# A 90 degree rotation in fp32: which engine makes the outputs of the first and the last macro tile

## Chip, cores, metric

One core of a Trainium2 chip. The metric is device time in microseconds (us) of one execution, the median of several runs. The core has TensorE (PE), VectorE (DVE), ScalarE (ACT), GpSimd (POOL), SyncE (SP) and 16 DMA engines.

## What is computed

```python
def setup_inputs():
    return {"x": np.random.randn(8192, 8192).astype(np.float32), "k": 1}

def reference(x, k):
    return np.rot90(x, k)
```

`out[i, j] = x[j, 8191 - i]`: a transpose with the order of the rows turned round. Nothing is calculated; 268 MB are read and 268 MB are written.

## The kernel before

**Tiling.** The input is cut into 16 macro tiles `kk` of 1024 rows (R) by 4096 columns (W). A macro tile has eight loads `t`, each 128 rows by 4096 columns (2 MB, load number `m = 8 kk + t`), and eight outputs `j`, each made of the 512 columns of chunk `j` of all eight loads (2 MB, output number `n = 8 kk + j`, stored as 512 rows by 1024 columns). Output `n` needs all eight loads of its macro tile.

**Stages.**
1. A load lands in one of five buffers. The first five loads use all five; after load 8 loads alternate between buffers 0 and 1 (`load_buf`), and the other three (2, 3, 4) are for outputs (`out_buf`). Loads 0 to 9 are issued by SP and ACT, all later ones by SP, each when DVE has turned the load that held its buffer before (`load_in_turn`, `taken`).
2. DVE turns the load into `ring`, which holds one macro tile, with the columns of each chunk in reverse order. Chunks that TensorE will transpose are copied (`tensor_copy`). The others are transposed in blocks of 32x32 (DVE's `transpose`, STREAM_TRANSPOSE in the profile). The last chunk of the last load (the corner) finds no slot in `ring`; it is turned into the landing buffer, and TensorE always transposes it. `pieces` lists in which portions and in what order DVE turns each load.
3. Outputs are made in one of two ways. `by_pe(kk)` names those that TensorE makes: 32 transposes of 128x128 into PSUM (two halves, `ps0` and `ps1`), which ACT copies into an output buffer. The others are `moved`: the 32x32 blocks are transposed already, and what is left are 16 copies that carry each row quadrant to its place (`moves`, `pairs`). DVE makes three of them (BY_DVE), POOL eight (BY_POOL) and ACT five; each is 32 partitions by 1024 elements.
4. ACT issues the store.

**Order.** Every engine has a fixed program, and the engines meet only in semaphores. DVE's program goes by loads: before it turns load `m` it makes its copies of output `n = m - 8`, if that is moved, and then waits for all of POOL's and its own copies of `n` (`s_pool`, `s_dve`), or for TensorE's transposes of `n` (`s_half`), since the load takes the places of output `n` in `ring`. POOL makes its eighth copy only when ACT has made all of its own (`s_act`). ACT stores a moved output when DVE has turned the first piece of load `n + 8`. An output buffer is written again only when its last store is done (`room_for`).

Macro tiles 1 to 12 (DVE, TensorE: 2 to 13) are played in a hardware loop two at a time, so in the profile most instructions have the line of a helper (L101, L104).

**Who makes what, before.** In macro tile 0 and in the last one, 15, TensorE makes all eight outputs. In macro tiles 1 to 13 it makes outputs 0 and 4, in 14 it makes 0, 2, 4, 6 and 7.

In the last macro tile no load follows that would need the ring, so the outputs are made in their order and ACT stores one after the other; outputs 120 and 121 are begun in halves before the last load is there (`FIRST`, `in_turn`).

Of the kernel before, what the change touches and what calls it, by code (L numbers as in the profile page):

```python
# [10 lines left out]
T = R // P  # L11
W = 4096
G = 4
J = W // (G * P)
# [7 lines left out]
Q = 32  # L22
BY_DVE = 3
BY_POOL = 8
BY_PE = [0, 4]
EARLY = range(T + 2)
BOTH = EARLY[-4:]
# [4 lines left out]
LAND = 2  # L32
OUTS = 3
# [140 lines left out]
def kernel(tc: tile.TileContext, x: bass.AP, k: bass.AP, out: bass.AP):  # L174
# [7 lines left out]
    KK = len(macros)  # L182
    n_out = KK * J
    n_load = KK * T
# [4 lines left out]
    wide = T // END  # L189
# [4 lines left out]
    outs = [(*o, [(j, g * P) for j in reversed(o[2]) for g in range(G)]) for o in outs]  # L194

    def by_pe(kk):
        if kk in (0, KK - 1):
            return list(range(J))
        return BY_PE if kk < KK - 2 else [*range(0, J, 2), J - 1]

    def in_quadrants(kk, j):
# [7 lines left out]
    for n, (kk, ts, js, blocks) in enumerate(outs):  # L209
# [5 lines left out]
        if kk < KK - 1 and js[0] == J - 1:  # L215
            ends = [F // H, F // H + rows, F]
# [24 lines left out]
    def moved_until(n):  # L241
        return sum(moved[: n + 1])
# [28 lines left out]
    def load_buf(m):  # L271
        if m < T:
            return m % (LAND + OUTS)
        return LAND + 2 if m == T else (m - T - 1) % LAND

    def out_buf(n):
        e = n - (KK * J - J)
        if e < 0:
            return LAND + (START if n < J else TURN[n // J % 2])[n % J]
        ends = [load_buf(n_load - 2)]  # L280
        ends += [LAND + i for i in reversed(range(OUTS))]
        ends += [load_buf(n_load - 1)]
        return ends[e % len(ends)]

    def once(e):
# [44 lines left out]
    for m in range(n_load):  # L330
        kk, t = divmod(m, T)
        here = by_pe(kk)
        rest = [j for j in range(J) if j not in here]
        if kk == KK - 1:
            got = [here] if t < T - 1 else [here[:wide], here[wide:-1], here[-1:]]
        elif t < T - 1:
            got = [here, rest]
        else:
            inner = [j for j in here if 0 < j < J - 1]
            got = [here[:1], [j for j in rest if j < J - 1], [J - 1], inner]  # L340
        got = [part for js in got for part in split(js)]
        pieces[m] = got
        for js in got:
            done += 1
            for j in js:
                rev[m, j] = done
# [6 lines left out]
    def landed(b, js):  # L353
        return at(bufs[b][:], (js[0] + 1) * CH - 1, [*strides(js, CH), [-1, CH]])

    def chunk(kk, t, js):
        if (kk, t, js[0]) == (KK - 1, T - 1, J - 1):
            return at(ring[:], 0, [[CH, 1], [1, CH]])
        places = [slot(kk, t, j) for j in js]
        assert max(places) < SLOTS  # L360
        return at(ring[:], places[0] * CH, [*strides(places, CH), [1, CH]])

    def moves(n, share):
        kk, ts, (j,), _ = outs[n]
        rows = len(ts) * P
        places = [slot(kk, t, j) for t in ts if (t, j) != (T - 1, J - 1)]
        ((step, tiles),) = strides(places, CH)
        for a, q in share:
            yield (
                at(  # L370
                    bufs[out_buf(n)][q * Q : q * Q + Q, :],
                    a * Q,
                    [[rows, G], [P, tiles], [1, Q]],
                ),
                at(
                    ring[a * Q : a * Q + Q, :],
                    places[0] * CH + q * Q,
                    [[P, G], [step, tiles], [1, Q]],
                ),
            )  # L380

    pairs = [(a, q) for a in range(P // Q) for q in range(P // Q)]

    def load(e, m, queue):
        r0, c0 = macros[m // T]
# [24 lines left out]
    def turned_in(n):  # L410
        kk, _, (j,), _ = outs[n]
        return rev[kk * T + T - 1 - (j == J - 1), j]
# [8 lines left out]
    def by_gpsimd(e):  # L421
        e.part(-1)
        e.memset(ident, 0.0).then_inc(s_id, 1)
        e.wait_ge(s_id, 1)
        e.affine_select(
            out=ident,
            in_=ident,
            compare_op=mybir.AluOpType.not_equal,
            fill=1.0,
            base=0,  # L430
            pattern=[[-1, P]],
            channel_multiplier=1,
        ).then_inc(s_id, 1)
        wait = once(e)
        for n, (kk, _, js, _) in enumerate(outs):
            e.part(kk)
            if moved[n]:
                room_for(wait, n)
                wait(s_rev, turned_in(n))
                for c, (to, of) in enumerate(moves(n, pairs[BY_DVE : BY_DVE + BY_POOL])):  # L440
                    if c == BY_POOL - 1:
                        wait(s_act, moved_until(n))
                    i = e.tensor_copy(out=to, in_=of)
                i.then_inc(s_pool, 1)

# [4 lines left out]
    def by_vector(e):  # L450
        wait = once(e)
        for m in range(n_load):
            kk, t = divmod(m, T)
            e.part(kk)
            b = load_buf(m)
            n = m - T
            if n >= 0 and moved[n]:
                room_for(wait, n)
                wait(s_rev, turned_in(n))
                for to, of in moves(n, pairs[:BY_DVE]):  # L460
                    i = e.tensor_copy(out=to, in_=of)
                i.then_inc(s_dve, 1)
            e.wait_ge(s_land[b], landings(m))
            if n >= 0:
                if moved[n]:
                    e.wait_ge(s_pool, moved_until(n))
                    e.wait_ge(s_dve, moved_until(n))
                else:
                    e.wait_ge(s_half, turned_until(n))
            for js in pieces[m]:  # L470
                if (m, js[0]) == (n_load - 1, J - 1):
                    e.wait_ge(s_half, turned_until(KK * J - J))
                if kk < KK - 1 and (t, js[0]) == (T - 1, J - 1):
                    wait(s_rev, rev[m, 0])
                    e.tensor_copy(
                        out=at(bufs[b][:], 0, [[CH, 1], [1, CH]]), in_=landed(b, js)
                    ).then_inc(s_rev, 1)
                    continue
                turn = e.transpose if in_quadrants(kk, js[0]) else e.tensor_copy
                turn(out=chunk(kk, t, js), in_=landed(b, js)).then_inc(s_rev, 1)  # L480

    def in_turn():
        for n in parts:
# [55 lines left out]
    def by_scalar(e):  # L539
        e.part(-1)  # L540
        wait = once(e)
        e.wait_ge(s_id, 2)
        e.copy(scratch, ident[:, :1])
        for m in EARLY[LAND + OUTS :]:
            load_in_turn(e, m, nc.scalar)
        for n, (kk, ts, js, blocks) in enumerate(outs):
            e.part(kk)
            r0, c0 = macros[kk]
            rows = len(ts) * P
            b = out_buf(n)  # L550
            if moved[n] or tight(n) or n == FIRST[1] or (kk < KK - 1 and js[0] == J - 1):
                room_for(wait, n)
            todo = list(moves(n, pairs[BY_DVE + BY_POOL :])) if moved[n] else []
            for to, of in todo[:1]:
                e.copy(to, of)
            if kk < KK - 1 and js[0] == J - 1:
                e.wait_ge(s_corner, kk + 1)
                e.copy(
                    at(bufs[b][:], rows - P, [[rows, G], [1, P]]),
                    at(corner, 0, [[P, G], [1, P]]),  # L560
                ).then_inc(s_freed, 1)
            if moved[n]:
                for to, of in todo[1:]:
                    i = e.copy(to, of)
                i.then_inc(s_act, 1)
                e.wait_ge(s_rev, rev[n + T, pieces[n + T][0][0]])
            else:
                for k, h, cols in parts[n]:
                    e.wait_ge(s_half, k + 1)
                    run, deep = len(cols) * P, 1  # L570
                    if cols[-1] - cols[0] >= run:
                        run = P * sum(f // rows == cols[0] // rows for f in cols)
                        deep = len(cols) * P // run
                    e.copy(
                        at(bufs[b][:], cols[0], [[rows, deep], [1, run]]),
                        at(ps[h][:], 0, [[run, deep], [1, run]]),
                    ).then_inc(s_ev, 1)
                e.wait_ge(s_ev, turned_until(n))
            groups = len(blocks)
            top = M - c0 - js[0] * CH - groups * P  # L580
            left = r0 + ts[0] * P
            e.dma_start(
                out=Place(out, top, groups * P, left, rows),
                in_=bufs[b][:, : groups * rows].rearrange("m (g f) -> m g f", f=rows),
            ).then_inc(s_store[b], 16)
# [50 lines left out]
```

## Time and profile before

| | |
|---|---|
| median of 3 runs (lowest, highest) | 1258.84 us (1258.72, 1259.64) |
| the profiled execution | 1259.08 us, of which 1257.8 us are the span of its instructions |
| DMA | 537.09 MB, 427 GB/s over the span |
| busy: DVE, POOL, ACT, PE | 63%, 59%, 48%, 24% of the span |
| loads | 128 of 2 MB (SP's queue q1, ACT's queue q10) |
| stores | 128 of 2 MB (ACT's queue q10), 15.8 us from issue to landing in the middle |

The page of the profile gives busy time by engine, then the span in 40 slices of 31.4 us, then the DMA queues, then the chain of work that ended last, followed back from the last instruction. "<-" names what ended an engine's idle time. In a row of the timeline the first number is the start and the second the time from the start of the group's first instruction to the end of its last, both in us; "x3" is how many instructions it merges; idle time before it stands in brackets. In a row of stretches the columns are: length, busy time of each engine with its instructions, TensorE's granted clock, DMA share (1 is all 16 DMA engines busy) and GB/s.

### The profile page before, as it was taken

What the parts mean: (1) busy time and instruction counts of PE and PEld (TensorE: products, weight loads), DVE (VectorE), ACT (ScalarE), POOL (GpSimd) and SP (SyncE); (2) the same over time, 40 slices, a digit from 0 to 9 for tenths busy, and PEclk for the clock granted to TensorE, in tenths of its full rate; (3) what the DMA queues carried; (4) which work ended last, traced back from release to release, by engine and by line L of the source; (5) the groups of instructions that cost most, each with busy time, mean ns of one, the idle gap of its engine ahead of it and who ended that gap; (6) DMA issues with size and microseconds to landing.
All of it is one profiled execution on the core that took longest, in us unless ns stands there. A gap on an engine that the chain in (4) does not pass through costs nothing.

```text
span 1257.8 us, 6012 instructions
## 1 busy us (share of the span) xinstructions
PE 302.9 (24%) x1556; PEld 264.8 (21%) x1556; DVE 793.8 (63%) x535; ACT 599.6 (48%) x556; POOL 744.0 (59%) x654
## 2 busy tenths in 40 slices
PE   1555013130131301313022130221302213024273
PEld 0454012130121301212012120121202212024273
DVE  2544866668666676666867667676677766764410
ACT  0334364463644636446364453645535455355364
POOL 0001966668666686666956668576685766965500
PEclk9987556555555555555556555565555556555597
DMA  9999999999999999999999999999999999999999
GB/s 400 420 430 429 429 429 429 429 431 430 430 430 429 430 428 430 428 430 430 430 430 429 431 428 431 428 430 428 430 430 429 430 429 431 427 423 428 427 428 381
DMA packets 36946, 537.09 MB, mean 427 GB/s; under 512 B 4160, under 2 KB 4160, under 8 KB 4160
## 3 DMA queue, kind: packets, MB, share of 16 engines
q10 hardware_dynamic: 19184, 278.93, 52.2%
q1 hardware_dynamic: 17744, 257.96, 48.0%
q8 instruction: 7, 0.11, 0.0%
q14 instruction: 11, 0.09, 0.0%
HBM read 268.44 MB, written 268.44 MB: 427 GB/s over the span
## 4 chain that ended last, share of the span: by engine, by line
DMA 71%; DVE 14%; ACT 4%; POOL 4%; issue 3%; PE 2%; ACTq 0%; DVEq 0%; SPq 0%; POOLq 0%
DMA buf<-in_x_dram 57%; DMA out_dram<-buf 14%; DVE ring L104 14%; ACT buf L104 4%; POOL buf L104 4%; PE ps L104 2%; ACTq L104 0%; DVE buf L104 0%; DVEq L101 0%; SPq L391 0%; DVEq L145 0%; POOLq L101 0%; SPq L311 0%; POOLq L151 0%; SPq L419 0%
## 5 line engine op out<-in xcount | busy, mean ns | idle before, releaser
L104 POOL COPY buf<-ring 32x1024 f32<-32x1024 f32 (+1 forms) x648 | 743.3, 1147 | 440.4 <-DMA out_dram<-buf 244.2
L104 ACT COPY buf<-ring 32x1024 f32<-32x1024 f32 (+1 forms) x405 | 414.8, 1024 | 324.2 <-DVE ring L104 292.5
L104 PE MATMUL ps<-head,ring 128*128 128x128 f32 x1496 | 290.7, 372 | 889.4 <-ACT buf L104 535.8
L104 PEld LDWEIGHTS ps<-head,ring 128*128 128x128 f32 x1496 | 255.3, 197 | 921.5 <-ACT buf L104 548.7
L104 DVE COPY ring<-buf 128x1024 f32<-128x1024 f32 (+5 forms) x152 | 157.7, 1044 | 415.6 <-DMA buf<-in_x_dram 320.1
L104 DVE STREAM_TRANSPOSE ring<-buf 128x3072 f32<-128x3072 f32 (+2 forms) x125 | 358.0, 2872 | 0.0
L104 ACT COPY buf<-ps 128x2048 f32<-128x2048 f32 (+4 forms) x149 | 183.3, 1278 | 313.6 <-DMA out_dram<-buf 149.3
L104 DVE COPY buf<-ring 32x1024 f32<-32x1024 f32 (+1 forms) x243 | 289.5, 1192 | 2.2
L104 PE MATMUL ps<-head,buf 128*128 128x128 f32 x60 | 15.2, 401 | 46.3 <-DVE buf L104 46.3
L104 PEld LDWEIGHTS ps<-head,buf 128*128 128x128 f32 x60 | 9.7, 199 | 52.0 <-issue 44.6
L104 DVE COPY buf<-buf 128x512 f32<-128x512 f32 x15 | 5.8, 387 | 0.0
L104 ACT ACT_TABLE_LOAD x1 | 1.3, 1283 | 3.4 <-PEq L419 3.4
L104 POOL MEMSET head<- 128x128 f32 x1 | 0.2, 204 | 2.9 <-POOLq L419 2.9
L104 POOL TENSOR_SCALAR_AFFINE_SELECT head<-head 128x128 f32<-128x128 f32 x1 | 0.3, 293 | 0.2 <-POOL head L104 0.2
L617 POOL MEMSET const-float32-0.0<- 128x1 f32 x1 | 0.1, 98 | 0.2 <-issue 0.2
L104 ACT COPY head<-head 128x1 f32<-128x1 f32 x1 | 0.2, 191 | 0.0
L617 POOL MEMSET const-bfloat16-1.0<- 128x1 bf16 x1 | 0.1, 100 | 0.0
L617 POOL MEMSET const-uint8-127<- 128x1 uint8 x1 | 0.1, 100 | 0.0
L617 POOL MEMSET const-float32-1.0<- 128x1 f32 x1 | 0.1, 98 | 0.0
## 6 DMA issues: line engine op xcount, KB each, us to landing
out_dram<-buf ACTq DMA_DIRECT2D x128, 2048.0 KB, 15.8
buf<-in_x_dram SPq DMA_DIRECT2D x121, 2048.0 KB, 15.0
buf<-in_x_dram ACTq DMA_DIRECT2D x3, 2048.0 KB, 16.9
buf<-in_x_dram SPq DMA_DIRECT2D x4, 1024.0 KB, 16.1
buf<-in_x_dram ACTq DMA_DIRECT2D x4, 1024.0 KB, 16.4
```

The lines of the kernel that those rows point to most:

```text
L104: i = getattr(e, self.name)(*self.args, **kwargs)
L617: nc = _bacc.Bacc("TRN2", target_bir_lowering=False, num_devices=1)
```

## The change

In macro tile 0 TensorE makes outputs 0 and 4 instead of all eight. In the last macro tile it makes outputs 0, 1, 3, 5 and 7; outputs 2, 4 and 6 become moved ones. For these three the 16 copies are shared out differently: DVE six, POOL six, ACT four. DVE makes them after its last load. POOL's last copy waits for ACT's and for DVE's, and ACT's store waits for POOL's. In the last macro tile the output buffers are taken in another order, so that output 2 goes into the buffer of the last load. `pieces` of the last load are cut accordingly: chunk 0, the other chunks of TensorE, the transposed chunks, chunk 7.

By the instruction lists of the two programs TensorE makes 188 transposes fewer in macro tile 0 and 96 fewer in the last one. Six outputs more in macro tile 0, and three more in the last, are made by 16 copies each.

```diff
+LAST_DVE = 6
+LAST_POOL = 6
+LAST_PE = [0, 1, 3, 5, 7]
...
     def by_pe(kk):
-        if kk in (0, KK - 1):
-            return list(range(J))
+        if kk == KK - 1:
+            return LAST_PE
         return BY_PE if kk < KK - 2 else [*range(0, J, 2), J - 1]
...
         ends = [load_buf(n_load - 2)]
-        ends += [LAND + i for i in reversed(range(OUTS))]
-        ends += [load_buf(n_load - 1)]
+        ends += [LAND + OUTS - 1, load_buf(n_load - 1)]
+        ends += [LAND + i for i in reversed(range(OUTS - 1))]
         return ends[e % len(ends)]
...
         if kk == KK - 1:
-            got = [here] if t < T - 1 else [here[:wide], here[wide:-1], here[-1:]]
+            got = [here, rest] if t < T - 1 else [here[:1], here[1:-1], rest, here[-1:]]
...
     pairs = [(a, q) for a in range(P // Q) for q in range(P // Q)]
+
+    def shares(n):
+        d, g = (BY_DVE, BY_POOL) if n < n_out - J else (LAST_DVE, LAST_POOL)
+        return pairs[:d], pairs[d : d + g], pairs[d + g :]
...
     def by_gpsimd(e):
...
-                for c, (to, of) in enumerate(moves(n, pairs[BY_DVE : BY_DVE + BY_POOL])):
-                    if c == BY_POOL - 1:
+                share = shares(n)[1]
+                for c, (to, of) in enumerate(moves(n, share)):
+                    if c == len(share) - 1:
                         wait(s_act, moved_until(n))
+                        if kk == KK - 1:
+                            wait(s_dve, moved_until(n))
                     i = e.tensor_copy(out=to, in_=of)
                 i.then_inc(s_pool, 1)
...
     def by_vector(e):
...
-                for to, of in moves(n, pairs[:BY_DVE]):
+                for to, of in moves(n, shares(n)[0]):
                     i = e.tensor_copy(out=to, in_=of)
                 i.then_inc(s_dve, 1)
...
+        for n in range(n_out - J, n_out):
+            if moved[n]:
+                room_for(wait, n)
+                wait(s_rev, turned_in(n))
+                for to, of in moves(n, shares(n)[0]):
+                    i = e.tensor_copy(out=to, in_=of)
+                i.then_inc(s_dve, 1)
...
     def by_scalar(e):
...
-            todo = list(moves(n, pairs[BY_DVE + BY_POOL :])) if moved[n] else []
+            todo = list(moves(n, shares(n)[2])) if moved[n] else []
...
                 i.then_inc(s_act, 1)
-                e.wait_ge(s_rev, rev[n + T, pieces[n + T][0][0]])
+                if kk < KK - 1:
+                    e.wait_ge(s_rev, rev[n + T, pieces[n + T][0][0]])
+                else:
+                    e.wait_ge(s_pool, moved_until(n))
```

## The prediction

> **What bounds the kernel now.** I read the page first (parts 2, 4 and 6), then stretches of 5 us at both ends, then the timeline of the first 53 us and of 122 to 160 us, where a later macro tile does what the first one is to do.
>
> ```profile
> DMA  9999999999999999999999999999999999999999
> GB/s 400 420 430 429 429 429 429 429 431 430 430 430 429 430 428 430 428 430 430 430 430 429 431 428 431 428 430 428 430 430 429 430 429 431 427 423 428 427 428 381
> ...
> DMA 71%; DVE 14%; ACT 4%; POOL 4%; issue 3%; PE 2%; ACTq 0%; DVEq 0%; SPq 0%; POOLq 0%
> ```
>
> The DMA engines are full from the first slice to the last. The kernel is bound by 537 MB at 430 GB/s, and an engine's time counts only if a queue runs empty over it. So the sum below asks one thing: when is the next transfer issued, and when does the DMA run out of earlier ones? A tile of 2.097 MB takes 2.097/0.430 = 4.88 us.
>
> ```profile
> core 0: us, PE busy (x) PEld busy (x) DVE busy (x) ACT busy (x) POOL busy (x), PEclk, DMA share, GB/s
> 0.00:60.00 60.00, 20.20 (x107) 16.08 (x108) 26.26 (x14) 12.76 (x11) 0.70 (x6) 1.00 0.98 409
> ...
> 1250.00:1255.00 5.00, 0.00 (x0) 0.00 (x0) 0.00 (x0) 0.00 (x0) 0.00 (x0) 0.50 0.88 374
> 1255.00:1257.80 2.80, 0.00 (x0) 0.00 (x0) 0.00 (x0) 0.00 (x0) 0.00 (x0) 0.50 0.07 29
> ```
>
> The DMA has moved 24.54 MB by 60.0. At the end the 16 engines stop on average at 1250 + 5 x 0.88 + 2.8 x 0.07 = 1254.6, but the span lasts to 1257.8: the slowest DMA engine runs about 3 us behind the mean. At 52 us the last of 16 arrivals of one transfer is only 0.24 us behind the first (arrivals in the trace).
>
> ```profile
> 42.31 0.43 DVE L104 COPY ring<-buf 128x512 f32<-128x512 f32 x1 [2.56 <-DMA buf<-in_x_dram]
> 45.87 0.64 ACTq L104 DMA_DIRECT2D out_dram<-buf  x1
> 47.22 0.69 DVE L104 COPY ring<-buf 128x1024 f32<-128x1024 f32 x1 [2.36 <-DMA buf<-in_x_dram]
> 47.83 3.37 DVE L104 STREAM_TRANSPOSE ring<-buf 128x3072 f32<-128x3072 f32 x1
> 53.27 0.58 ACTq L104 DMA_DIRECT2D out_dram<-buf  x1
> ```
>
> Before, DVE waits for the DMA at load 7 (42.31), and stores 0 and 1 go out at 45.87 and 53.27.
>
> ```profile
> 132.43 0.69 DVE L104 COPY ring<-buf 128x1024 f32<-128x1024 f32 x1 [0.93 <-POOL buf L104]
> 133.16 0.55 ACTq L104 DMA_DIRECT2D out_dram<-buf  x1
> 142.68 0.69 DVE L104 COPY ring<-buf 128x1024 f32<-128x1024 f32 x1 [2.00 <-POOL buf L104]
> 146.58 4.34 DVE L104 COPY buf<-ring 32x1024 f32<-32x1024 f32 x3
> 152.93 0.69 DVE L104 COPY ring<-buf 128x1024 f32<-128x1024 f32 x1 [2.00 <-POOL buf L104]
> 168.16 2.03 DVE L104 COPY buf<-ring 32x1024 f32<-32x1024 f32 x3
> ```
>
> This is what an output made from 32x32 copies costs in the second macro tile: DVE waits for POOL at 132.43, 142.68 and 152.93, so POOL needs 10.25 us for its eight copies of one output. In that time the DMA moves a load and a store, 9.76 us. POOL is slower than the DMA by 0.5 us per output; there, earlier stores in the queue hide it. The first output, begun by POOL at 122.38, took 10.05.
>
> **The change part by part.**
>
> *Step 1, turning in the first macro tile.* A load is turned by one 1024 copy and one 3072 transpose, 47.22 to 51.20 = 3.98 us, where a 4096 copy takes 2.29. Loads 4 and 5 are there at 32.60; back to back DVE ends load 4 at 36.6, load 5 at 40.6, load 6 at 44.5. Load 7 (landed by 42.31) starts at 44.5, 2.2 us late. Its pieces take 3.9 (the same five in the next macro tile, 112.57 to 116.45), and its corner chunk comes after the transposes. There the first store followed the start by 117.92 - 112.57 = 5.35: store 0 goes out at 49.9, 4.0 us later.
>
> *Step 2, the loads behind them.* Loads 8, 9 and 10 wait for loads 4, 5 and 6: issued at 36.5, 40.5 and 44.6 (before 34.9, 37.1, 39.8). The queues carry loads until about 51, so all stand in line in time: 0 us. If that line were shorter by 3 us, load 10 would leave a hole of as much in SP's queue, which a store then fills.
>
> *Step 3, output 1 becomes a POOL output.* POOL may start when load 7 is turned and its corner is through TensorE, 4.4 us after 44.5: 48.9. It ends 10.0 later, 58.9. DVE, in order, waits for it before it turns load 9, and ACT's store waits for that first piece (0.8 us, 132.43 to 133.16): store 1 at 59.7, before 53.27. Queued behind the wait on DVE: load 9, and with it SP's load 11 (63.1, before 56.8).
>
> *Step 4, where the DMA runs out.* Issued by then are loads 0 to 10 and store 0, twelve tiles, 25.17 MB. From the row above: 60.0 + 0.62/0.43 = 61.4. After that there is nothing until store 1 starts.
>
> *Step 5, the holes.* How long from an issue to the first packet is the uncertain price. With idle DMA engines the trace has 1.05 us (the first load, 0.91 to 1.96); behind running traffic 3.45 (load issued at 168.26 into an empty queue, first packet 171.75). I take 1.05 behind whatever is left in line, at most 3.45. Store 1: 61.4 + 1.05 = 62.5, a hole of 1.05. Store 2 is issued 10.25 later, 69.95; the DMA is out at 62.5 + 9.76 + 0.3 = 72.6 (0.3 for slow first packets: the stretch 50 to 55, where the first store begins, is 0.5 us short); it starts at 73.4, a hole of 0.85. Store 3 at 80.2, out at 83.5, start 83.7: 0.2. Sum 2.1, less 0.2 that the slowest DMA engine lies behind: **+1.9**. With 1.05 throughout, the holes end at 80.2 + 1.05 against 81.0: 0.3. With 3.45 throughout: 2.0 + 0.5 + 0.5, 3.0.
>
> *Step 6, outputs 4 to 7 and the loop.* Output 4 stays with TensorE and its store follows 4.3 us behind store 3; load 13 follows at about 84. The line is full again, and from output 5 on buffers come free as in the second macro tile: 0. Were one of the three further copied outputs to open a hole, it would be one more of 0.5.
>
> *Step 7, turning in the last macro tile.* A load costs 0.69 + 1.22 + 1.77 = 3.7 instead of 2.29 to 2.9, so SP's loads go out about 1.4 later; but ACT's stores of the copied outputs 113, 115 and 117 wait for the first piece alone and go out 1.6 earlier. DMA share stays 0.99 to 1.02 there. 0, bounds -1 and +1.
>
> *Step 8, the last stores.* Before, ACT issues stores 121 to 127 every 4.26 us and the DMA needs 4.88, so a line builds up. Now output 122 starts at 1213.0 (load 127 fully turned), DVE's six copies at 1.45 (4.34/3) end at 1221.7, POOL's last copy follows with about 1.1, store 122 at 1223. Then 3.64 + 0.6 for TensorE's 123 (1227), four ACT copies 4.2, one on POOL and the store (1233) for 124, and so on: 1237, 1243, and 1247.6 for 127 (before 1240.86). The DMA would reach 122 at 1254.6 - 6 x 4.88 = 1225.3, and 124 at 1235.1. The mean engine has 1.5 to 2.3 us in hand, the slowest 3 more, and that one sets the end: 0, bounds 0 and +2.
>
> *Step 9, what is taken away.* TensorE makes 188 transposes fewer in the first macro tile and 96 fewer in the last. TensorE is 24% busy and off the path: 0 for these. Its program is shorter, and loads of instructions (page part 3, q8, seven) take one DMA engine about 1 us each: bounds -2 and 0. I take 0.
>
> The profiled execution took 1259.08 at a span of 1257.8; the sum gives 1261.0. It stands 0.24 above the median of 1258.84, so the forecast is **1260.8 us**.
>
> **The rivals.**
>
> *No hole opens (chance 0.10, about 1259).* The line before store 1 is only 1.7 us short of hiding it; stores that start faster than 1.05 would close it. The Trainium skill, DMA: Bandwidth & Descriptors, § Latency and other measured facts, gives about 600 ns to the first byte on these queues; by that store 1 starts at 60.3, store 3 at 80.8, both before the DMA runs out, and the sum is 0. This trace's shortest is 1.05 and its usual one 3.45, so I give it little.
>
> *POOL is slower than 10.25 per output, and the copied outputs set the pace of the first macro tile (chance 0.30, about 1265, slower).* Its place is outputs 1 to 3. At 1138.11 eight POOL copies took 11.63 us while DVE copied beside them. At 11.6 each, store 3 goes out at 48.9 + 34.8 + 0.8 = 84.5 instead of 80.2: 4.3 more. It decides from about 10.45: then 3 x 0.2 brings the loss over 2.5. For it: DVE now has no idle time between its copies. Against it: three outputs in a row took 10.25 under the same load. The Trainium skill, SBUF — State Buffer, § Who interferes with whom, says that DVE's copies in a two-port mode and GpSimd hold a shared port pair in turn, each for the whole instruction. By that an output costs 8 x 1.03 + 3 x 0.68 + 0.69 = 10.97, and store 3 would go out 2.4 later than I have it; the measured period of 10.25 is shorter than that.
>
> *The last stores run dry (chance 0.10, about 1263.5, slower).* If DVE's and POOL's copies of output 122 take 12 instead of 9.9 and the slowest DMA engine is not behind (it lags 3 us now, but how much at 1225 hangs on chance loads), step 8 costs 2 to 3 on top.
>
> *Faster by over 2.5 us (chance 0.06, about 1256).* Only the lag of the slowest DMA engine (3 us) and step 9 could give it; no engine's work is on the path.
>
> **How the numbers follow.** 0.2% is 2.5 us, about what a measurement of this kernel can tell from no change. The forecast case has 0.44, of which 0.06 lies beyond 2.5 us (latency 3.45 throughout). Slower: 0.06 + 0.30 + 0.10 = 0.46, of which I put 0.02 back for POOL only just over its point: 0.44. Faster 0.06. Same: 0.50. The range goes from the case with no hole and a little of step 9 (1257.8) to POOL at 11.6 (1265). The likeliest case's own range is 1259.1 to 1261.9.
>
> **What would show it.** In the profile after: store 0 near 50, store 1 near 60, DVE waiting for POOL at about 59, 69 and 79; stretches 60:65, 70:75 and 80:85 with a DMA share under 1 (5 us less 1.05 is 0.79); stretches after 90 full. Store 127 near 1248 plus the shift and still a full DMA share until about 1255. It is wrong if the share never falls at 60 to 85 (no hole), if POOL's period there is over 10.5, or if the share falls after 1220.

## The result, and the profile after

The changed kernel takes 1260.89 us in the median of 22 runs (1259.83 to 1263.56), the kernel before 1258.92 (1258.47 to 1259.64, 22 runs). The ratio is 1.0016, 95% interval 1.001 to 1.0021: slower by 2.0 us, clear of noise, and inside the 0.2% that the prediction counts as no change. The profiled execution took 1260.51 us at a span of 1259.2.

The page of the changed kernel: GB/s in 40 slices, the queues that load instructions, and the chain that ended last.

```profile
GB/s 399 415 407 425 429 429 430 430 427 430 431 428 430 428 430 430 428 430 428 431 430 429 430 430 429 430 429 430 430 429 430 428 431 429 429 426 430 429 427 384
...
q8 instruction: 5, 0.08, 0.0%
...
DMA 71%; DVE 15%; POOL 4%; ACT 4%; issue 3%; PE 2%; DVEq 0%; ACTq 0%; SPq 0%; POOLq 0%
```

The kernel is still bound by the DMA, and 36 of the 40 slices are within 3 GB/s of before. The second, third and fourth slice (31 to 126 us) fell from 420, 430 and 429 to 415, 407 and 425. To size that, the same stretches of both kernels; the columns are length, busy time of PE, PEld, DVE, ACT and POOL, TensorE's clock, DMA share and GB/s. First the kernel before:

```profile
50.00:60.00 10.00, 6.35 (x51) 5.40 (x50) 5.18 (x3) 6.94 (x6) 0.00 (x0) 0.98 1.01 408
60.00:70.00 10.00, 6.93 (x40) 6.30 (x39) 3.98 (x2) 3.79 (x3) 0.00 (x0) 0.68 1.00 429
70.00:80.00 10.00, 5.79 (x36) 5.26 (x34) 3.98 (x2) 3.79 (x3) 0.00 (x0) 0.83 1.01 431
80.00:125.00 45.00, 25.63 (x143) 21.96 (x141) 18.40 (x13) 18.07 (x16) 2.54 (x3) 0.77 1.00 428
```

Then the changed kernel:

```profile
50.00:60.00 10.00, 3.17 (x15) 2.94 (x15) 8.93 (x6) 5.78 (x6) 9.65 (x9) 0.84 1.00 383
60.00:70.00 10.00, 1.13 (x6) 1.13 (x7) 8.99 (x6) 5.21 (x5) 9.65 (x9) 0.50 1.00 388
70.00:80.00 10.00, 1.91 (x9) 1.50 (x8) 8.99 (x6) 5.20 (x5) 9.15 (x8) 0.50 1.01 418
80.00:125.00 45.00, 11.19 (x53) 9.92 (x54) 28.37 (x22) 23.96 (x23) 26.52 (x25) 0.58 1.00 423
...
125.00:1257.00 1132.00, 240.39 (x1157) 212.18 (x1155) 783.49 (x539) 564.99 (x532) 763.85 (x666) 0.56 1.01 429
```

Bytes not moved, in time at 430 GB/s: (408 - 383) x 10/430 = 0.6 us, (429 - 388) x 10/430 = 1.0, 13 x 10/430 = 0.3 and 5 x 45/430 = 0.5, together 2.4 us. After 125 us nothing more is lost: by the packets of the trace the changed kernel is 1.00 MB behind at 125 us and 0.96 MB at 1100 us. The two profiled spans differ by less, 1.4 us; the slowest of the 16 DMA engines ends a span, and where in these two executions it made up the rest is not shown. The split over the four stretches is that of one execution. The kernel of the first experiment below has the same first macro tile, and there nothing is lost from 50 to 60 us and 1.4 from 60 to 70; the sum is 2.4 again.

The DMA share stays at 1.00: in this execution the 16 engines were seldom idle, their packets took longer. Of the packets of 16 KB, 0.611 us each as a rule, 116 between 40 and 92 us took more than 0.7 us (before 29), the longest 1.4 (before 1.2). Per engine the packets took 2.6 us longer than they would at 0.611 each (before 0.8), and the engine was idle 0.3 us more than before.

The timeline of the changed kernel, first column the start:

```profile
47.54 0.38 DVE L107 COPY buf<-buf 128x512 f32<-128x512 f32 x1
...
49.24 30.20 POOL L107 COPY buf<-ring 32x1024 f32<-32x1024 f32 x24 [45.11 <-PE ps L107]
...
50.60 0.65 ACTq L107 DMA_DIRECT2D out_dram<-buf  x1
...
59.36 1.55 DVE L107 COPY ring<-buf 128x1024 f32<-128x1024 f32 x1 [0.99 <-POOL buf L107]
60.84 3.36 DVE L107 STREAM_TRANSPOSE ring<-buf 128x3072 f32<-128x3072 f32 x1
60.95 0.58 ACTq L107 DMA_DIRECT2D out_dram<-buf  x1
...
69.45 1.56 DVE L107 COPY ring<-buf 128x1024 f32<-128x1024 f32 x1 [0.99 <-POOL buf L107]
71.04 0.55 ACTq L107 DMA_DIRECT2D out_dram<-buf  x1
...
79.53 0.69 DVE L107 COPY ring<-buf 128x1024 f32<-128x1024 f32 x1 [0.99 <-POOL buf L107]
```

POOL makes outputs 1, 2 and 3 without a break from 49.24 on (24 copies in 30.20 us), DVE waits for it at 59.36, 69.45 and 79.53, and the stores go out right behind. SP's load 11, which waits for the same DVE piece, goes out at 64.23 (before 56.80).

### The profile page after: what moved, and what is told of

Read it like the earlier page. It is cut to its first block, busy times and chain, and to the rows that moved or that the text cites. A ratio compares the mean times of both kernels' runs of the same rounds, so it can differ in the third digit from the quotient of the medians.

```text
span 1259.2 us, 5582 instructions
## 1 busy us (share of the span) xinstructions
PE 267.8 (21%) x1272; PEld 234.2 (19%) x1272; DVE 869.9 (69%) x595; ACT 609.8 (48%) x574; POOL 820.3 (65%) x720
## 4 chain that ended last, share of the span: by engine, by line
DMA 71%; DVE 15%; POOL 4%; ACT 4%; issue 3%; PE 2%; DVEq 0%; ACTq 0%; SPq 0%; POOLq 0%
DMA buf<-in_x_dram 54%; DMA out_dram<-buf 16%; DVE ring L107 15%; POOL buf L107 4%; ACT buf L107 4%; PE ps L107 2%; DVEq L104 0%; ACTq L107 0%; SPq L398 0%; DVE buf L107 0%; SPq L426 0%; SPq L314 0%; POOLq L104 0%; SPq L421 0%
## 5 line engine op out<-in xcount | busy, mean ns | idle before, releaser
L107 POOL COPY buf<-ring 32x1024 f32<-32x1024 f32 x714 | 819.6, 1148 | 421.1 <-ACT buf L107 179.9
L107 ACT COPY buf<-ring 32x1024 f32<-32x1024 f32 (+1 forms) x447 | 458.0, 1025 | 353.8 <-DVE ring L107 318.4
L107 PE MATMUL ps<-head,ring 128*128 128x128 f32 x1212 | 255.6, 393 | 926.9 <-ACT buf L107 539.4
L107 PEld LDWEIGHTS ps<-head,ring 128*128 128x128 f32 x1212 | 224.8, 210 | 954.3 <-ACT buf L107 553.0
L107 DVE COPY ring<-buf 128x1024 f32<-128x1024 f32 (+3 forms) x159 | 147.5, 935 | 365.5 <-DMA buf<-in_x_dram 259.4
L107 DVE STREAM_TRANSPOSE ring<-buf 128x3072 f32<-128x3072 f32 (+1 forms) x142 | 398.5, 2814 | 0.0
L107 DVE COPY buf<-ring 32x1024 f32<-32x1024 f32 (+1 forms) x279 | 337.5, 1210 | 2.7
L107 ACT COPY buf<-ps 128x512 f32<-128x512 f32 (+3 forms) x125 | 150.3, 1249 | 282.0 <-DMA out_dram<-buf 144.6
```

Source lines behind the costliest of these rows:

```text
L107: i = getattr(e, self.name)(*self.args, **kwargs)
```

## Experiments

Two theories stood at the start. **A:** the loss is in the first macro tile, where stores and loads go out late and the DMA's queues run out. **B:** it is at the end, where the last store goes out 8 us later (1249.12, before 1240.86). "Over before" is always the difference of medians (11 runs of the experiment) to the kernel before, run beside it on the same chip. The intervals of the ratios are about 0.0009 to either side, 1.1 us, so a difference of 0.5 us is not told from none, and neither are the 0.6 and 0.8 us between some of the experiments and the changed kernel; there the bytes moved say more than the times.

### One half of the change at a time

First macro tile alone:

```diff
     def by_pe(kk):
-        if kk in (0, KK - 1):
+        if kk == KK - 1:
             return list(range(J))
```

> Only the first macro tile is changed (outputs 0 and 4 by TensorE), the last one is as before. Theory A (all of the loss of about 2.0 us is in the first macro tile, where stores 0 to 3 go out late and a DMA queue runs empty): +1.8 to +2.4 us over the kernel before, bytes moved by 125 us about 1.0 MB behind. Theory B (the loss is at the end, where the last store goes out 8 us later): 0 to +0.5 us. Theory C (half and half): about +1.

Last macro tile alone (the changed kernel, with):

```diff
     def by_pe(kk):
+        if kk == 0:
+            return list(range(J))
         if kk == KK - 1:
             return LAST_PE
```

> Only the last macro tile is changed (outputs 0, 1, 3, 5 and 7 by TensorE), the first one is as before. Theory A: -0.4 to +0.3 us against the kernel before, although store 127 goes out about 6 us later. Theory B: +1.5 to +2.0 us. Theory C: about +1.

First alone: 1261.0 against 1258.9, +2.1 us (ratio 1.0016, 1.0007 to 1.0026). Last alone: 1258.38, -0.5 (0.9996, 0.9987 to 1.0005). Theory B falls, and theory A stands: the loss is made in the first macro tile. That the last macro tile alone gains 0.5 is not shown, its interval holds 1. The kernel with the first half alone, in the two stretches that matter:

```profile
50.00:60.00 10.00, 3.46 (x15) 3.06 (x15) 8.99 (x6) 5.65 (x6) 9.65 (x9) 1.00 1.02 413
60.00:70.00 10.00, 1.66 (x8) 1.67 (x9) 8.99 (x6) 5.21 (x5) 9.65 (x9) 1.00 0.94 367
```

Here the DMA share does fall, to 0.94 (0.86 from 60 to 65), where the changed kernel's stays at 1.00. Slow packets are the larger part here too: 2.6 us per engine from 40 to 92 us, as in the changed kernel, and 0.6 us more idle time than before. So the loss shows mostly as slow packets and in part as idle engines; GB/s shows both.

At the end the changed half really delays the stores. The last one of the kernel with the last half alone, on ACT's queue:

```profile
1243.74 3.63 ACT L107 COPY buf<-ps 128x2048 f32<-128x2048 f32 x2 [1.71 <-POOL buf L107]
1247.40 0.55 ACTq L107 DMA_DIRECT2D out_dram<-buf  x1
```

It goes out 6.5 us later than before and the span is 1257.3 (before 1257.8): the line of stores covers it.

### Which of the delays in the first macro tile

Store 0 earlier: DVE turns load 7's corner chunk ahead of the 32x32 transposes.

```diff
             got = [here[:1], [j for j in rest if j < J - 1], [J - 1], inner]
+            if kk == 0:
+                got = [got[0], got[2], got[1], got[3]]
```

> The changed kernel, but of load 7 DVE turns the corner chunk before the 32x32 transposes, not after, so that store 0 goes out about 2.9 us earlier (about 47.7 instead of 50.6) and store 1 about 0.9 earlier. Theory A: about 0.5 to 1.0 us faster than the changed kernel, that is +1.0 to +1.5 over the kernel before, and the stretch 50 to 55 near 387 GB/s instead of 354. Theory B (the loss is at the end): no difference from the changed kernel (+2.0).

POOL faster: it makes 7 of the 16 copies in the first macro tile, ACT 6.

```diff
         d, g = (BY_DVE, BY_POOL) if n < n_out - J else (LAST_DVE, LAST_POOL)
+        if n < J:
+            d, g = 3, 7
```

> The changed kernel, but in the first macro tile POOL makes 7 of the 16 copies of an output and ACT 6 (DVE 3 as before). POOL's period falls from 10.1 to about 9.3 us, below the 9.76 us in which the DMA moves a load and a store; stores 1, 2 and 3 go out at about 59.3, 68.6 and 78 instead of 60.95, 71.0 and 80.3. Theory A with POOL's period as its cause: 0.7 to 1.2 us faster than the changed kernel (+0.8 to +1.3 over the kernel before). Theory A with only the late first store as its cause: about as the changed kernel (+1.7 to +2.1).

Store 1 earlier: TensorE makes output 1 of the first macro tile as well.

```diff
+        if kk == 0:
+            return [0, 1, 4]
         return BY_PE if kk < KK - 2 else [*range(0, J, 2), J - 1]
```

> The changed kernel, but in the first macro tile TensorE makes outputs 0, 1 and 4. Store 1 no longer waits for POOL (about 58 instead of 60.95), and POOL starts on output 2 when load 8 is turned, about 54 (store 2 about 65 instead of 71.0). Theory A (the loss is the time by which stores 1 to 3 are late): 0.8 to 1.3 us faster than the changed kernel, +0.7 to +1.2 over the kernel before. Rival (the 32x32 transposes on DVE and the late store 0 do it, which stay): +1.7 to +2.1.

The first two edits together, and all three:

> The changed kernel with both edits of the runs before in the first macro tile: the corner chunk of load 7 first, and 7 copies on POOL and 6 on ACT. The first alone was 0.6 us and the second 0.8 us faster than the changed kernel. If the two are separate parts of the loss they add up: about 1259.4, +0.4 to +0.8 over the kernel before. If both act through the same late store 1 they do not: about 1260.0.

> As the run before, and TensorE makes outputs 0, 1 and 4 of the first macro tile. Theory A: stores 0 to 3 are then about as early as in the kernel before, the loss in the first macro tile is 0 to 0.5 us and the last macro tile gains 0.5: 1258.3 to 1259.0, the same as the kernel before or as the kernel with only the last macro tile changed (1258.38). If 32x32 transposes in the first macro tile cost something by themselves: 1259.5 or more.

All in one table: issue of store 1 and of load 11 and GB/s from 40 to 125 us (one profiled execution each), and the time (medians).

| kernel | store 1 | load 11 | GB/s 40:125 | over before, us |
|---|---|---|---|---|
| before | 53.27 | 56.8 | 425 | 0 |
| changed | 60.95 | 64.2 | 414 | +2.0 |
| first macro tile alone | 60.82 | 64.1 | 414 | +2.1 |
| corner first | 60.19 | 63.5 | 416 | +1.4 |
| POOL 7, ACT 6 | 60.36 | 63.6 | 418 | +1.2 |
| corner first, and POOL 7, ACT 6 | 58.83 | 62.1 | 423 | -0.3 |
| output 1 by TensorE | 57.59 | 60.1 | 426 | -0.6 |
| all three | 54.93 | 58.7 | 426 | -0.3 |

In bytes, (425 - GB/s) x 85/430, the kernels have lost 2.2 us with store 1 at 60.95 and 60.82, 1.8 at 60.19, 1.4 at 60.36, 0.4 at 58.83 and nothing at 57.59 and 54.93. So the loss starts where store 1 goes out at about 58.5, with load 11 some 3 us behind it, and each further us costs about one. That is 2.9 us ahead of 61.4, the prediction's point at which the DMA has nothing left. The table can't say which of the late transfers counts: load 11 and stores 2 and 3 move with store 1.

With each of the first two edits the time fell by about as much as expected (0.6 and 0.8 us), but the steps between did not go as expected. With the corner first, the stretch 50 to 55 stayed at 347 GB/s, although store 0 went out at 47.94. With 7 copies on POOL, store 1 went out at 60.36 and not at 59.3, since POOL's last copy had to wait for ACT, which had six to make and begins them behind store 0:

```profile
49.18 7.14 POOL L107 COPY buf<-ring 32x1024 f32<-32x1024 f32 x6 [45.05 <-PE ps L107]
57.65 6.79 POOL L107 COPY buf<-ring 32x1024 f32<-32x1024 f32 x6 [1.33 <-ACT buf L107]
```

With the corner first, store 0 and ACT's copies come 2.9 us earlier and that wait is gone. So the two edits together move store 1 by 2.1 us, where alone they move it by 0.8 and 0.6, and they took 2.25 us off (1258.64), not the 1.4 or less that I had expected. All three together gave 1258.60, as expected.

Output 1 on TensorE takes the whole loss away (1258.34), not the half of it that I had expected. It leaves most of the 32x32 transposes in place, and store 0 is still late (49.53), so these two cost nothing that shows. Stores 2 and 3 stay with POOL, but they too go out about 5 us earlier (66.24 and 75.47). In the profile of the kernel with output 1 by TensorE, stores 0 and 1 and POOL's start on output 2:

```profile
49.53 0.65 ACTq L107 DMA_DIRECT2D out_dram<-buf  x1
...
53.04 7.93 POOL L107 COPY buf<-ring 32x1024 f32<-32x1024 f32 x7 [48.90 <-DVE ring L107]
...
56.14 0.69 DVE L107 COPY ring<-buf 128x1024 f32<-128x1024 f32 x1 [3.17 <-PE ps L107]
57.59 0.58 ACTq L107 DMA_DIRECT2D out_dram<-buf  x1
```

DVE turns load 9 at 56.14, released by TensorE, instead of 59.36, released by POOL.

### A late store or load by itself

Was it store 1, the loads, or both together? Each was delayed alone, in the kernel before. Store 1 alone:

```diff
             groups = len(blocks)
+            if n == 1:
+                e.wait_ge(s_land[load_buf(T + 2)], landings(T + 2))
```

> The kernel before, but ACT waits with store 1 until load 10 has landed, about 62.5 instead of 53.27, that is later than in the changed kernel (60.95); DVE and POOL are as before, so load 11 goes out as before at about 57. Theory H (the loss arises only where both queues run out, store 1 and load 11 late together): 0 to +0.5 us. Rival (a late store 1 costs by itself): +1.5 to +2.5 us.

Store 1 went out at 64.22, 3.3 us later than in the changed kernel, with load 11 at 57.06 as before. Time 1259.11 against 1258.82, +0.3 (ratio 1.0001, 0.9992 to 1.001), at 422 GB/s from 40 to 125 (0.6 us in bytes). A late store 1 by itself does not cost 1.5; that agrees with the theory that it takes an end of both lines. Load 11 late by itself was not tried in the first macro tile.

Loads alone, ten times in the middle of the kernel before:

```diff
         taken(e.wait_ge, last[-1])
+        if m % T == 3 and 3 <= m // T <= 12:
+            e.wait_ge(s_dve, moved_until(m - T - 1))
```

> The kernel before, but ten loads (the fourth of macro tiles 3 to 12) wait in addition until DVE has made its three copies of the output that follows, so they are issued about 4.4 us later, SP's queue is empty for about that long ten times, and ACT's queue with its stores has the DMA alone. Theory H (only a time in which both queues are empty costs): 0 to +1 us. Theory R (a queue that starts again after it was empty makes all 16 DMA engines slow for a packet, though the other queue has work): 0.3 to 0.8 us each time, +3 to +8 us, with no lower DMA share but fewer GB/s.

Time 1258.47 against 1258.90, -0.4 (0.9997, 0.9988 to 1.0006). The delay was smaller than planned: no packet of SP's queue ran for 1.2 to 1.8 us before each of the ten loads. The stretch from 250 to 1100 us, with nine of them, where the kernel before has 430:

```profile
250.00:1100.00 850.00, 161.33 (x730) 141.75 (x730) 562.19 (x406) 419.68 (x401) 587.05 (x526) 0.54 1.01 429
```

A queue that runs empty and starts again costs nothing that the time shows, as long as the other queue has work. In bytes this kernel is 0.32 MB behind the one before from 200 to 1000 us, 0.07 us for each restart. The rival, 0.3 to 0.8 us for each, is excluded: ten would have cost 3 to 8.

### Whether the last macro tile gains by earlier stores

In the kernel with the last half alone, ACT issues stores 113, 115 and 117 1.7 to 1.9 us earlier (1150.87, 1170.65 and 1190.09 against 1152.63, 1172.56 and 1191.77), as step 7 had it. The kernel before with this alone:

```diff
-            got = [here] if t < T - 1 else [here[:wide], here[wide:-1], here[-1:]]
+            got = [here[:1], here[1:]] if t < T - 1 else [here[:wide], here[wide:-1], here[-1:]]
```

> The kernel before, but in the last macro tile DVE turns chunk 0 of each load as a piece of its own ahead of the other seven, so that ACT's stores of the copied outputs 113, 115 and 117, which wait for the first piece, go out about 1.7 us earlier, as they do when only the last macro tile is changed. If that is where the 0.5 us come from by which that kernel was faster than the kernel before: 0.3 to 0.6 us faster. If they come from fewer TensorE instructions to be fetched, or are chance: -0.2 to +0.2.

1258.81 against 1258.82. In its profile the three stores were at 1151.85, 1172.23 and 1190.94, at most 0.8 us earlier, so the test is weak. What the 0.5 us of the last half come from, if they are real, stays open.

## Why the prediction was right

The forecast was 1260.8 and the median is 1260.89. Direction, place and size were right, and the result lies in the likeliest case's own range. The form of the loss was not: the prediction has the DMA idle until the next first packet comes, and says that it is wrong if the share never falls from 60 to 85. In the changed kernel's profile the share of every 5 us there is between 0.98 and 1.04. The bytes are missing all the same, in the stretches that it named. By the steps:

- **Step 1 and 2, turning:** store 0 at 50.60 (49.9 forecast), loads 8, 9 and 10 at 36.8, 40.7 and 44.5 (36.5, 40.5, 44.6). Right. In the changed kernel's profile 0.6 us are lost from 50 to 60, but the late store 0 is not shown to cost them: with the first macro tile alone it is as late (50.47) and nothing is lost there.
- **Step 3, output 1 on POOL:** POOL began at 49.24 and DVE was released at 59.36 (48.9 and 58.9 forecast). Store 1 went out at 60.95, not 59.7. The terms that were mis-sized are POOL's end, by 0.46, and DVE's first piece: 1.55 us and not 0.69. At both places POOL starts its next output in the same moment. In the changed kernel its copy started 0.03 us ahead of DVE's and DVE's took long; at 132.43, the row that the prediction goes by, DVE's started first, and POOL's took long. Of the rows, the first two are of the changed kernel, the other two of the kernel before:

```profile
59.33 1.03 POOL L107 COPY buf<-ring 32x1024 f32<-32x1024 f32 x1
59.36 1.55 DVE L107 COPY ring<-buf 128x1024 f32<-128x1024 f32 x1 [0.99 <-POOL buf L107]
...
132.43 0.69 DVE L104 COPY ring<-buf 128x1024 f32<-128x1024 f32 x1 [0.93 <-POOL buf L104]
132.46 1.57 POOL L104 COPY buf<-ring 32x1024 f32<-32x1024 f32 x1
```

- **Step 4, where the DMA runs out:** 61.4. In the changed kernel load 10 landed at 60.05 and store 0 at 63.12, so for most of 60 to 63 a single transfer was left. By the table of experiments an issue has to come about 2.9 us ahead of 61.4 to cost nothing.
- **Step 5, the holes:** the sum 2.1, less 0.2, against 2.4 us of bytes and +2.0 in time. The parts differ: nothing, 1.05, 0.85 and 0.2 forecast for the four stretches, 0.6, 1.0, 0.3 and 0.5 in the changed kernel's profile, and 0, 1.4, 0.3 and 0.8 in that of the first macro tile alone. First packets came 1.24, 1.70 and 2.58 us after the issue of stores 1, 2 and 3 (62.20, 72.74, 82.84), inside the bounds of 1.05 and 3.45. Most of the loss came as slow packets and not as idle engines, so "a DMA share under 1" was the wrong sign to look for; GB/s was the right one. The step's upper case has a slip: 59.7 + 3.45 - 61.4 is 1.75 and not 2.0, which makes its sum 2.7 and not 3.0.
- **Step 6 to 9:** from 80 to 125 us 0.5 are lost in the changed kernel's profile (0 forecast, 0.5 if one output opened a hole). The last stores ran late as worked out (127 at 1249.12; 1247.6 and the shift forecast) and cost nothing. Instruction loads fell from seven to five without a gain that shows.

That the total came out to 0.1 us is therefore partly luck: store 1 was 1.25 us later than forecast, its first packet came before store 0 had ended (62.20 and 63.12), and the loss came as slow packets that no step has. What carried the forecast was the question asked of every delay, whether the DMA still has something in line.

**The rivals.** "No hole opens" fell in what it stands for, no loss: the changed kernel lost 2.4 us of transfers, if hardly as idle time. The 600 ns of the Trainium skill (DMA: Bandwidth & Descriptors, § Latency and other measured facts) would have led there; here 1.05 to 2.58 us were measured. "POOL is slower" fell as well: its period was 10.1 us (59.36, 69.45, 79.53), below its point of 10.45; the 10.97 by an exclusive port pair (the Trainium skill, SBUF — State Buffer, § Who interferes with whom) was too high. The engines do seem to take turns, as the rows at 59.33 and 132.43 show, but a copy's whole recorded time is not exclusive (last section). "The last stores run dry" fell with the run of the last half alone (-0.5). A gain of over 2.5 us did not come.

No kernel here beats the kernel before by more than the interval of its ratio. The lowest are 1258.34 (output 1 of the first macro tile by TensorE too) and 1258.38 (last half alone).

## What to carry to other kernels

Where transfers bind, a change off the path is judged by one sum: what is issued so far, how long the DMA works on it, and when the next transfer is issued. In this kernel that line was short at the start, so a slower but elsewhere harmless way of making an output cost there alone; it was enough to keep one output on the fast engine. A delay counts only beyond what the line hides, so a cure is judged by when the next transfer goes out. Two edits can look weak singly, each held up by what the other removes, and be nearly complete together.

## What had not been expected of the hardware

- A thin line of transfers shows as slow packets, up to 1.4 us instead of 0.611, with a DMA share of 1.00. Why the packets slow down there is not settled. When SP's queue alone was idle for 1.2 to 1.8 us there were few of them: 41 over 0.7 us from 250 to 1100 us, before 7.
- DVE's and POOL's 32x1024 copies hold each other up, but not for all of their time. Alone they take 0.68 us on DVE and 1.03 on POOL, 1.71 in turn. Where both copy without a break, as here in the changed kernel's first macro tile, one of each takes 1.44 us: DVE's copy ends 0.55 us after POOL's of before (55.51 to 56.94, behind one that ended at 56.39), and POOL's next ends 0.89 after that:

```profile
55.51 1.43 DVE L107 COPY buf<-ring 32x1024 f32<-32x1024 f32 x1
56.43 1.40 POOL L107 COPY buf<-ring 32x1024 f32<-32x1024 f32 x1
56.95 1.43 DVE L107 COPY buf<-ring 32x1024 f32<-32x1024 f32 x1
```
